# Attention scores on TensorE: the second matmul of two neighbouring key chunks on 64 rows each, in different halves of the array

## The chip, the cores and the metric

The kernel runs on one core of a Trainium2 chip. The metric is the device time of one execution in microseconds; lower is better. Before the change three runs took 1370.55 to 1374.48 us, median 1372.14 us. The profile shows one execution of its own, which took 1372.62 us.

## What is computed

The reference is one layer of a mixed encoder: a normalised input of 2048 tokens by 1024 channels, one input projection to 4364 columns, three groups that read it (a matrix-memory group of 4 heads, a forgetting attention of 4 heads with 64 channels each, a convolution group), a gate for each, an output projection, a residual and a final norm. The change lies in the attention:

```
cum    = cumsum(log_sigmoid(f_pre))                  # per head, over tokens
logits = q @ k.T * 64**-0.5 + cum[query] - cum[key]  # causal, 128-query blocks
p      = softmax(logits)
y      = p @ v
```

## The kernel before

The work is written per 512 tokens (`TB`), as blocks 0 to 3. For each block the input is normalised and transposed, and the projections run as matmuls whose operands are split in two parts, `hi` (the value in the matmul's 32-bit format `F32R`) and `lo` (what is left). Three products (hi hi, hi lo, lo hi) are added in PSUM. The weights are read again from DRAM for each block.

**How the attention's operands are laid out.** `unit_fqk` (line 382) projects q and k of a block, splits them into `hi` and `lo` and stores both to DRAM scratch, `q_d` and `k_d`. `k_d[head, part, 64, token]` holds for each head 64 rows of `hi` and then 64 rows of `lo`. `fox_load_qk` (line 813) reads back: a key chunk of 512 tokens is a tile of 128 rows, `hi` in rows 0 to 63 and `lo` in rows 64 to 127. The queries come as two tiles: `L["q", 0]` has q's `hi` twice, once in each half of the rows, and `L["q", 1]` has q's `lo` twice.

**The scores.** `fox_scores` (line 850) works on 128 queries (`qi`) of a pair of such blocks (`pr`) against all key chunks that they may see: 1 chunk for queries of block 0, up to 4 for block 3. For each chunk one PSUM tile `pq` receives two matmuls of 128 rows: L864 with q's `hi` (so hi hi + hi lo) and L865 with q's `lo` (so lo hi + lo lo). VectorE then adds the forgetting bias and keeps the running maximum (L872), which frees the PSUM tile, and GpSimd masks the bias of the chunk on the diagonal (L869). After the last chunk ScalarE takes the exponentials (L879). The diagonal chunk has only the columns that the queries can see, rounded up to at least 256.

`fox_scores` is a generator that yields once per chunk. `fox_run` (line 953) advances it one or two items ahead of `fox_apply` (line 887), which transposes the probabilities on TensorE (L918), splits them (L926, L927) and multiplies by the values (L905, L906). While the last projections of block 3 are made, `fox_run` is stepped from inside them (`bg_step`, line 267); afterwards it is the main loop, and the output projection `outproj` (L1063) is stepped from a counter (`FR`, line 1165) as filler. A planner with a cost model of its own then orders the instructions of each engine; among those that can run, those written earlier go first.

**PSUM.** Eight banks: pool `psp` has 3 (tag "p": `pq` of query blocks 2 and 3, and the output projection's `po`), `psx` has 2, `psm` has 3 (tag "m": `pq` of query blocks 0 and 1, and the transposes `ptr`).

Of the kernel before, what the change touches and what calls it, by code (L numbers as in the profile page):

```python
# [8 lines left out]
F32 = mybir.dt.float32  # L9
F32R = mybir.dt.float32r  # L10
AF = mybir.ActivationFunctionType
ALU = mybir.AluOpType
# [4 lines left out]
P = 128  # L17
S = 2048
# [3 lines left out]
TB = 512  # L22
# [5 lines left out]
NEG = -1e30  # L28
# [10 lines left out]
def tile_hybrid_trunk(  # L39
# [21 lines left out]
    v, s, g, pe, dma = nc.vector, nc.scalar, nc.gpsimd, nc.tensor, nc.sync  # L61
# [16 lines left out]
    k_d = scratch.tile([H, 2, 64, S], F32, name="k_d")  # L78
# [37 lines left out]
    psp = ps1.enter_context(tc.tile_pool(name="psp", bufs=PB[0], space=PSUM))  # L116
    psx = ps1.enter_context(tc.tile_pool(name="psx", bufs=PB[1], space=PSUM))
    psm = ps1.enter_context(tc.tile_pool(name="psm", bufs=PB[2], space=PSUM))
# [132 lines left out]
    def load_unit(name):  # L251
        if len(uready) < 2:
            prefetch()
        for _ in range(min(TP, len(backlog))):
            backlog.pop(0)()
        run_stage()
        if side:
            side.pop(0)()
        nm, w = uready.pop(0)
        assert nm == name  # L260
        return w
# [18 lines left out]
    def mm_cm(name, w, h, m):  # L280
        ps = proj_psum(f"pc_{name}")
        cs = slice(m * P, (m + 1) * P)
        n = 0
        for k in range(KT):
            wh, wl = w[0][k // 4][:, k % 4, cs], w[1][k // 4][:, k % 4, cs]
            for a, r in ((wh, h[0][k]), (wh, h[1][k]), (wl, h[0][k])):
                pe.matmul(ps, a, r, start=(n == 0), stop=(n == 3 * KT - 1))  # L287
                n += 1
            bg_step()
        return ps  # L290
# [91 lines left out]
    def unit_fqk(b, h, which):  # L382
        w = load_unit(f"f{which}{b}")
        for m in range(2):
            ps = mm_cm(f"f{which}{b}_{m}", w, h, m)
            lo = cpool.tile([P, 542], F32R, name=f"ql{which}{b}{m}", tag="c")[:, 0:TB]
            qf = lo.bitcast(F32)
            if which == 0:
                s.activation(qf, ps, AF.Identity, bias=colse[:, m : m + 1], scale=0.125)
            else:  # L390
                s.activation(qf, ps, AF.Identity, bias=cols[:, R_BFQ + 2 + m : R_BFQ + 3 + m])
            hi = cpool.tile([P, 542], F32R, name=f"qh{which}{b}{m}", tag="c")[:, 0:TB]
            s.copy(hi, qf)
            v.tensor_tensor(lo, qf, hi.bitcast(F32), op=ALU.subtract)
            bs = slice(b * TB, (b + 1) * TB)
            for e, t in enumerate((hi, lo)):
                if which == 0:
                    dma.dma_start(q_d[m, e, :, bs], t.bitcast(F32))
                else:
                    for a in range(2):  # L400
                        dma.dma_start(k_d[2 * m + a, e, :, bs], t[a * 64 : (a + 1) * 64, :].bitcast(F32))

    def silu2(name, ps, bcol, pool, tag, bufs):
        o = pool.tile([P, 542], F32, name=f"o_{name}", tag=tag, bufs=bufs)[:, 0:TB]
# [445 lines left out]
    def fox_scores(qd, hd, pr, L, out_):  # L850
        nk = qd * TB + (pr + 1) * 256
        nch = qd + 1
        for qi in range(2):
            t0 = qd * TB + pr * 256 + qi * P
            nm = f"{qd}{hd}{pr}{qi}"
            qs = slice(pr * 256 + qi * P, pr * 256 + (qi + 1) * P)
            mx = fpool.tile([P, 16], F32, name=f"mx{nm}", tag="mx", bufs=MXB)
            Sc = []
            for ch in range(nch):
                W = min(TB, nk - ch * TB)  # L860
                Wq = W if ch < qd else W - P * (1 - qi)
                pq = (psm if qd < PQM else psp).tile([P, 512], F32, name=f"pq{nm}{ch}", tag="m" if qd < PQM else "p")
                Wm = max(Wq, 256)
                pe.matmul(pq[:, 0:Wm], L["q", 0][:, qs], L["k", ch][:, 0:Wm], start=True, stop=False)  # L864
                pe.matmul(pq[:, 0:Wm], L["q", 1][:, qs], L["k", ch][:, 0:Wm], start=False, stop=True)  # L865
                nb = L["n", ch]
                if ch == qd:
                    nb = fpool.tile([P, TB], F32, name=f"nd{nm}", tag="nd", bufs=NDB)
                    g.affine_select(out=nb[:, 0:Wq], in_=L["n", ch][:, 0:Wq], pattern=[[-1, Wq]],  # L869
                                    compare_op=ALU.is_ge, fill=NEG, base=t0 - ch * TB, channel_multiplier=1)  # L870
                Sb = fpool.tile([P, TB], F32, name=f"S{nm}{ch}", tag="S", bufs=SB)
                v.tensor_tensor_reduce(  # L872
                    Sb[:, 0:Wq], pq[:, 0:Wq], nb[:, 0:Wq], 1.0,
                    NEG if ch == 0 else mx[:, ch - 1 : ch], ALU.add, ALU.max, mx[:, ch : ch + 1])
                Sc.append((Sb, Wq))
                yield
            v.tensor_scalar(mx[:, 4:5], mx[:, qd : qd + 1], -1.0, None, op0=ALU.mult)  # L877
            for ch, (Sb, Wq) in enumerate(Sc):
                s.activation(Sb[:, 0:Wq], Sb[:, 0:Wq], AF.Exp, bias=mx[:, 4:5], accum_out=mx[:, 8 + ch : 9 + ch])  # L879
            sm = mx[:, 8:9]  # L880
            if nch > 1:
                sm = mx[:, 5:6]
                v.reduce_sum(sm, mx[:, 8 : 8 + nch], axis=AX.X)
            v.reciprocal(mx[:, 6:7], sm)
            out_.append(([t for t, _ in Sc], mx))
# [62 lines left out]
    L, SH = {}, {}  # L948
# [4 lines left out]
    def fox_run(items, on_item=lambda i: None):  # L953
# [11 lines left out]
        def advance(i):  # L965
            load(nqk, fox_load_qk, min(i + (AH0 if items[min(i, len(items) - 1)][0] < 2 else AH), len(items) - 1 if free_hh else 15))
            if i < len(items) and i not in gens:
                qd, hp, hh, pr = items[i]
                ress[i] = []
                gens[i] = fox_scores(qd, hp * 2 + hh, pr, L[qd, hp, hh], ress[i])  # L970
# [106 lines left out]
    for b in range(NB):  # L1077
# [35 lines left out]
        if b < NB - 1:  # L1113
            unit_fz(b, h)
            conv_fin(b, h, accs)
            hn = hprep(b + 1)
            unit_fqk(b, h, 0)
            unit_fqk(b, h, 1)
            h = hn
# [10 lines left out]
    fpool = ctx.enter_context(tc.tile_pool(name="fpool", bufs=2, side="right"))  # L1130
# [5 lines left out]
    for k in range(EP):  # L1136
        prep_out(k)
    unit_fqk(b, h, 0)
    for k in range(EP, 4):
        prep_out(k)  # L1140
# [7 lines left out]
    def fillers():  # L1148
        for qd in range(NB):
            while ODONE[qd] not in marks:  # L1150
                yield
            yield from outproj(qd)

    fill = fillers()
    k = 4
    f = 0.0
# [21 lines left out]
NDB = 2  # L1178
SB = 12
# [9 lines left out]
PQM = 2  # L1189
# [49 lines left out]
```

## Time and profile before

| | |
|---|---|
| median of 3 runs | 1372.14 us |
| the profiled execution | 1372.62 us |
| its span in the profile | 1370.8 us |
| TensorE (PE) busy | 1278.7 us, 93% of the span, 7383 matmuls |
| weight loads (PEld) busy | 1112.9 us, 81% |
| VectorE (DVE) busy | 961.0 us, 70% |
| ScalarE (ACT) busy | 570.3 us, 42% |
| GpSimd (POOL) busy | 345.1 us, 25% |
| score matmuls L864 and L865 | 160 each, from 912.9 us to 1297.3 us |

A timeline row gives the start, the duration, the engine, the line, the tiles, the shape of the array used (rows * columns), the shape written and how many instructions were merged into the row. A matmul needs its weight load (PEld) first. Durations of matmuls overlap, since the array is pipelined: what one costs is the distance between two starts.

### The profile page before, as it was taken

What the parts mean: (1) busy time and instruction counts of PE and PEld (TensorE: products, weight loads), DVE (VectorE), ACT (ScalarE), POOL (GpSimd) and SP (SyncE); (2) the same over time, 40 slices, a digit from 0 to 9 for tenths busy, and PEclk for the clock granted to TensorE, in tenths of its full rate; (3) what the DMA queues carried; (4) which work ended last, traced back from release to release, by engine and by line L of the source; (5) the groups of instructions that cost most, each with busy time, mean ns of one, the idle gap of its engine ahead of it and who ended that gap; (6) DMA issues with size and microseconds to landing.
All of it is one profiled execution on the core that took longest, in us unless ns stands there. A gap on an engine that the chain in (4) does not pass through costs nothing. (4 is left out here: it accounts for less than half of the span.)

```text
span 1370.8 us, 21119 instructions
## 1 busy us (share of the span) xinstructions
PE 1278.7 (93%) x7383; PEld 1112.9 (81%) x7383; DVE 961.0 (70%) x2473; ACT 570.3 (42%) x1204; POOL 345.1 (25%) x398
## 2 busy tenths in 40 slices
PE   3747999999999999999999999998989999999997
PEld 2637898887889888989888889988868888878886
DVE  6789948748997655794662796674786677866742
ACT  4472434354233236330314232224575565655631
POOL 3466545510132010050110070121131211211121
PEclk9977999999999999999999999999999999999999
DMA  9947768699897469564558764469986454644141
GB/s 266 321 170 235 239 231 292 230 320 397 305 347 246 155 221 314 186 214 167 188 189 270 217 242 173 168 228 326 294 263 183 152 173 143 198 149 134 62 131 62
DMA packets 151874, 301.62 MB, mean 220 GB/s; under 512 B 14968, under 2 KB 92072, under 8 KB 133592
## 3 DMA queue, kind: packets, MB, share of 16 engines
q1 hardware_dynamic: 151768, 300.28, 65.4%
q8 instruction: 58, 0.95, 0.3%
q14 instruction: 48, 0.39, 0.1%
HBM read 224.54 MB, written 75.69 MB: 219 GB/s over the span
## 5 line engine op out<-in xcount | busy, mean ns | idle before, releaser
L461 DVE SCALAR_TENSOR_TENSOR ac<-ca,dww,ac 128x512 f32<-128x512 f32 x228 | 181.5, 831 | 2.4 <-ACT ac L446 1.9
L1063 PE MATMUL po<-wo,yh 128*128 128x512 f32 x512 | 164.7, 397 | 1.0 <-ACT yh L1053 0.7
L287 PE MATMUL pc_qk<-hh,w_qk 128*128 128x512 f32 x512 | 163.1, 395 | 0.3 <-DMA w_qk<-wd_qk 0.3
L299 PE MATMUL pt_mv<-w_mv,hh 128*128 128x256 f32 (+1 forms) x512 | 100.4, 297 | 29.2 <-ACT w_mv L181 10.5
L879 ACT ACTIVATE S<-S,mx 128x512 f32<-128x512 f32 (+3 forms) x160 | 103.7, 651 | 52.4 <-DVE mx L877 48.8
L287 PEld LDWEIGHTS pc_qk<-hh,w_qk 128*128 128x128 f32 x512 | 96.2, 188 | 21.0 <-DMA w_qk<-wd_qk 0.6
L1063 PEld LDWEIGHTS po<-wo,yh 128*128 128x128 f32 x512 | 94.1, 188 | 21.0 <-ACT yh L1053 0.9
L299 PEld LDWEIGHTS pt_mv<-w_mv,hh 128*128 128x128 f32 x512 | 84.7, 202 | 31.1 <-ACT w_mv L181 10.9
L927 DVE TENSOR_TENSOR tl<-ptr,th 128x512 fp32r<-128x512 f32 (+1 forms) x144 | 92.4, 654 | 24.7 <-ACT th L926 23.7
L1063 PE MATMUL po<-wo,ya 128*128 128x512 f32 x256 | 101.1, 396 | 0.0
L299 PE MATMUL pt_mo<-w_mo,hh 128*128 128x256 f32 x512 | 96.9, 290 | 4.3 <-DMA w_mo<-wd_mo 2.2
L287 PE MATMUL pc_qk<-hl,w_qk 128*128 128x512 f32 x256 | 100.8, 394 | 0.0
L926 ACT CAST th<-ptr 128x512 fp32r<-128x512 f32 (+1 forms) x144 | 76.3, 561 | 51.2 <-PE ptr L918 50.3
L552 DVE SCALAR_TENSOR_TENSOR am<-um,cols,am 128x512 f32<-128x512 f32 x96 | 83.4, 877 | 10.1 <-ACT am L549 9.3
L918 PE MATMUL ptr<-ident,S 128*128 128x128 f32 x544 | 84.1, 275 | 4.8 <-DVE tl L927 3.4
L299 PEld LDWEIGHTS pt_mo<-w_mo,hh 128*128 128x128 f32 x512 | 82.0, 196 | 4.8 <-DMA w_mo<-wd_mo 2.4
L287 PE MATMUL pc_f<-hh,w_f 128*128 128x512 f32 x256 | 84.8, 400 | 0.0
L869 POOL TENSOR_SCALAR_AFFINE_SELECT nd<-n 128x128 f32<-128x128 f32 (+1 forms) x64 | 30.5, 479 | 208.4 <-DVE mx L872 129.0
L287 PE MATMUL pc_mz<-hh,w_mz 128*128 128x512 f32 x256 | 82.7, 395 | 0.0
L299 PE MATMUL pt_mv<-w_mv,hl 128*128 128x256 f32 (+1 forms) x256 | 74.7, 293 | 0.0
L299 PE MATMUL pt_mo<-w_mo,hl 128*128 128x256 f32 x256 | 73.4, 289 | 0.0
L918 PEld LDWEIGHTS ptr<-ident,S 128*128 128x128 f32 x544 | 64.5, 142 | 10.1 <-DVE tl L927 2.8
(267 smaller groups left out, 3245.0 us busy)
## 6 DMA issues: line engine op xcount, KB each, us to landing
w_qk<-wd_qk SPq DMA_DIRECT2D x24, 1024.0 KB
w_mo<-wd_mo SPq DMA_DIRECT2D x12, 1024.0 KB
w_mz<-wd_mz SPq DMA_DIRECT2D x12, 1024.0 KB
w_f<-wd_f SPq DMA_DIRECT2D x12, 1024.0 KB
w_mv<-wd_mv SPq DMA_DIRECT2D x10, 1024.0 KB
n<-nb_d SPq DMA_DIRECT2D x36, 256.0 KB
wa<-in_w_ada_dram SPq DMA_DIRECT2D x16, 512.0 KB
x<-in_x_dram SPq DMA_DIRECT2D x16, 512.0 KB
```

The lines of the kernel that those rows point to most:

```text
L287: pe.matmul(ps, a, r, start=(n == 0), stop=(n == 3 * KT - 1))
L299: pe.matmul(ps[:, 0:width], a[:, cs], r, start=(n == 0), stop=(n == 3 * KT - 1))
L461: backlog.append(lambda acc=acc, u=u, i=2 * j + m, j=j: v.scalar_tensor_tensor(acc, u[:, j : j + TB], dww[:, i : i + 1], acc, op0=ALU.mult ...
L552: v.scalar_tensor_tensor(acc, u[:, j : j + TB], cols[:, r + 8 * j : r + 8 * j + 1], acc, op0=ALU.mult, op1=ALU.add)
L869: g.affine_select(out=nb[:, 0:Wq], in_=L["n", ch][:, 0:Wq], pattern=[[-1, Wq]], compare_op=ALU.is_ge, fill=NEG, base=t0 - ch * TB, channel ...
L879: s.activation(Sb[:, 0:Wq], Sb[:, 0:Wq], AF.Exp, bias=mx[:, 4:5], accum_out=mx[:, 8 + ch : 9 + ch])
L918: pe.transpose(pt[:, i, qi * P : (qi + 1) * P], Ps[qi][0][kk // TB][:, kk % TB : kk % TB + P], ident)
L926: s.copy(f(th), f(pt))
L927: v.tensor_tensor(f(tl), f(pt), f(th.bitcast(F32)), op=ALU.subtract)
L1063: pe.matmul(po, a, w[:, ns], start=(i == 0), stop=(i == 3 * KT - 1))
```

## The change

Two things change.

- In `unit_fqk` the keys of odd blocks are stored with the parts exchanged: `lo` in rows 0 to 63 and `hi` in rows 64 to 127. For even blocks nothing changes.
- In `fox_scores` the chunks are taken two at a time. First both chunks get their matmul with q's `hi` on all 128 rows, as before. Then both get their second matmul, now on only the 64 rows that hold the key's `hi` part: rows 0 to 63 for the even chunk, rows 64 to 127 for the odd one. These two use different halves of the array's rows and different PSUM tiles. The product lo lo is left out there. A chunk without a partner (the only chunk of query block 0, the third of block 2) keeps both matmuls of 128 rows. The mask, the bias and the maximum of both chunks follow after all four matmuls, with one yield each as before.

```diff
@@ unit_fqk
-                        dma.dma_start(k_d[2 * m + a, e, :, bs], t[a * 64 : (a + 1) * 64, :].bitcast(F32))
+                        dma.dma_start(k_d[2 * m + a, e ^ (b % 2), :, bs], t[a * 64 : (a + 1) * 64, :].bitcast(F32))
@@ fox_scores
-            for ch in range(nch):
-                W = min(TB, nk - ch * TB)
-                Wq = W if ch < qd else W - P * (1 - qi)
-                pq = (psm if qd < PQM else psp).tile([P, 512], F32, name=f"pq{nm}{ch}", tag="m" if qd < PQM else "p")
-                Wm = max(Wq, 256)
-                pe.matmul(pq[:, 0:Wm], L["q", 0][:, qs], L["k", ch][:, 0:Wm], start=True, stop=False)
-                pe.matmul(pq[:, 0:Wm], L["q", 1][:, qs], L["k", ch][:, 0:Wm], start=False, stop=True)
-                nb = L["n", ch]
...
-                yield
+            for c0 in range(0, nch, 2):
+                grp = []
+                for ch in range(c0, min(c0 + 2, nch)):
+                    W = min(TB, nk - ch * TB)
+                    Wq = W if ch < qd else W - P * (1 - qi)
+                    pq = (psm if qd < PQM else psp).tile([P, 512], F32, name=f"pq{nm}{ch}", tag="m" if qd < PQM else "p")
+                    Wm = max(Wq, 256)
+                    pe.matmul(pq[:, 0:Wm], L["q", 0][:, qs], L["k", ch][:, 0:Wm], start=True, stop=False)
+                    grp.append((ch, Wq, Wm, pq))
+                for ch, Wq, Wm, pq in grp:
+                    r = slice(0, P) if len(grp) == 1 else slice(64 * (ch % 2), 64 * (ch % 2) + 64)
+                    pe.matmul(pq[:, 0:Wm], L["q", 1][r, qs], L["k", ch][r, 0:Wm], start=False, stop=True)
+                for ch, Wq, Wm, pq in grp:
+                    nb = L["n", ch]
...
+                    yield
```

The lines left out (mask, bias, maximum) are the same on both sides.

More of the change, by code (lines that the diff above doesn't have):

```diff
@@ L858, in fox_scores @@
             Sc = []
-            for ch in range(nch):
-                W = min(TB, nk - ch * TB)
-                Wq = W if ch < qd else W - P * (1 - qi)
-                pq = (psm if qd < PQM else psp).tile([P, 512], F32, name=f"pq{nm}{ch}", tag="m" if qd < PQM else "p")
-                Wm = max(Wq, 256)
-                pe.matmul(pq[:, 0:Wm], L["q", 0][:, qs], L["k", ch][:, 0:Wm], start=True, stop=False)
-                pe.matmul(pq[:, 0:Wm], L["q", 1][:, qs], L["k", ch][:, 0:Wm], start=False, stop=True)
-                nb = L["n", ch]
[L867 to L875, printed above, removed]
-                yield
@@ new lines, in fox_scores @@
+            for c0 in range(0, nch, 2):
[12 more added lines that the diff above has]
+                    nb = L["n", ch]
+                    if ch == qd:
+                        nb = fpool.tile([P, TB], F32, name=f"nd{nm}", tag="nd", bufs=NDB)
+                        g.affine_select(out=nb[:, 0:Wq], in_=L["n", ch][:, 0:Wq], pattern=[[-1, Wq]],
+                                        compare_op=ALU.is_ge, fill=NEG, base=t0 - ch * TB, channel_multiplier=1)
+                    Sb = fpool.tile([P, TB], F32, name=f"S{nm}{ch}", tag="S", bufs=SB)
+                    v.tensor_tensor_reduce(
+                        Sb[:, 0:Wq], pq[:, 0:Wq], nb[:, 0:Wq], 1.0,
+                        NEG if ch == 0 else mx[:, ch - 1 : ch], ALU.add, ALU.max, mx[:, ch : ch + 1])
+                    Sc.append((Sb, Wq))
+                    yield
```

## The prediction

> **What bounds the kernel now.** First the busy time of each engine, then the same by stretches of the part that the change touches.
>
> ```profile
> span 1370.8 us, 21119 instructions
> PE 1278.7 (93%) x7383; PEld 1112.9 (81%) x7383; DVE 961.0 (70%) x2473; ACT 570.3 (42%) x1204; POOL 345.1 (25%) x398
> ```
> ```profile
> 950.00:1000.00 50.00, 46.35 (x276) 39.41 (x275) 34.21 (x126) 29.03 (x76) 10.26 (x31) 0.97 0.88 280
> 1000.00:1050.00 50.00, 44.98 (x256) 36.47 (x256) 39.23 (x138) 31.68 (x83) 15.19 (x29) 1.00 0.70 218
> 1050.00:1100.00 50.00, 50.00 (x298) 43.71 (x297) 33.49 (x96) 28.83 (x73) 9.32 (x17) 1.00 0.57 175
> 1100.00:1150.00 50.00, 49.34 (x298) 43.15 (x297) 36.56 (x110) 29.12 (x74) 10.58 (x21) 1.00 0.59 175
> 1200.00:1250.00 50.00, 46.77 (x274) 40.92 (x273) 33.41 (x94) 27.30 (x70) 6.74 (x13) 0.97 0.43 130
> 1250.00:1300.00 50.00, 49.66 (x297) 43.24 (x296) 35.77 (x99) 30.19 (x75) 8.72 (x15) 1.00 0.34 103
> ```
>
> The columns are PE, PEld, DVE, ACT, POOL, then the granted clock, the DMA share and GB/s. TensorE is busy for 45 to 50 us of every 50 at full clock, VectorE for 33 to 39. What TensorE waits for between 1000 and 1300 us, by the view of waits, and the last long step of the chain that ends last:
>
> ```profile
> PE pq L864 <- DVE mx L872: 4.8, 5, 2.8
> PE pa L905 <- ACT th L926: 1.4, 3, 0.6
> PE ptr L918 <- DVE tl L927: 1.1, 2, 1.0
> ```
> ```profile
> 1324.05 39.62 PE po L1063 x171
> ```
>
> These three are 7.3 us in 300. From 1000 us to the end the kernel is a queue of matmuls, and the last of them end it: a microsecond more or less of TensorE work in the scores is nearly a microsecond of time. The chain's row also prices a matmul of 512 columns in that queue: 39.62 / 171 = 0.232 us.
>
> **What the change removes.** The number of matmuls and loads stays: 160 of L864, 160 of L865.
>
> ```profile
> L865 PE MATMUL pq<-k,q x112: 274/393/632, 1021.6 to 1297.3; 128*128 128x512 f32 x88, 128*128 128x256 f32 x16, 128*128 128x384 f32 x8
> L865 PE MATMUL pq<-kv,q x48: 277/389/522, 913.1 to 1029.9; 128*128 128x512 f32 x24, 128*128 128x256 f32 x16, 128*128 128x384 f32 x8
> ```
>
> A set of 128 queries occurs 16 times per query block (4 heads, 2 `pr`, 2 `qi`). Block 0 has no pair, block 1 has one per set, block 2 one (its third chunk is single), block 3 two: 64 pairs. In 32 of them both chunks are full; in the 32 of chunks (0,1) of block 1 and (2,3) of block 3 the second is the diagonal one, 256 columns wide in 16, 384 in 8, 512 in 8. If both halves run at once, the shorter matmul of the pair disappears. Its price by width, from starts that follow each other:
>
> ```profile
> 1122.67 0.28 PE L906 MATMUL pa<-tl,v 128*128 128x256 f32 x1
> 1122.79 0.28 PE L905 MATMUL pa<-th,v 128*128 128x256 f32 x1
> ```
> ```profile
> 963.60 0.34 PE L864 MATMUL pq<-kv,q 128*128 128x384 f32 x1
> 963.78 0.34 PE L865 MATMUL pq<-kv,q 128*128 128x384 f32 x1
> ```
>
> So 0.12 us and 0.18 us. Removed at most: 40 x 0.232 + 8 x 0.18 + 16 x 0.12 = **12.6 us**. The halves still need a load each. In the row of four loads below, 0.47 us with 0.14 for the last, loads follow each other by 0.11 us. If the upper half's load comes after the lower half's, its matmul starts up to 0.11 us late: nothing is lost with a partner of 256 columns (0.11 + 0.12 = 0.23), 0.06 with 384, 0.11 with 512, together 40 x 0.11 + 8 x 0.06 = 4.9 us. I take that loss, since nothing else is ahead of the two loads to hide them (next part): **7.7 us removed**, bounds 0 (the halves run one after the other) and 12.6.
>
> **What it adds: changing the rows in use, twice per pair.** No score matmul of before uses 64 rows. But the trace has one instruction on fewer than 65 rows inside a busy stretch, a transpose of 62 rows (L793), between one of 74 rows and projection matmuls of 128:
>
> ```profile
> 62.76 0.14 PEld L792 LDWEIGHTS pt_cols<-ident,r 74*128 74x128 f32 x1
> 62.87 0.23 PE L792 MATMUL pt_cols<-ident,r 74*128 74x74 f32 x1
> 63.03 0.14 PEld L793 LDWEIGHTS pt_cols<-ident,r 62*128 62x128 f32 x1
> 63.03 0.27 PE L793 MATMUL pt_cols<-ident,r 62*128 62x62 f32 x1
> 63.23 0.30 PEld L299 LDWEIGHTS pt_v<-w_v,hl 128*128 128x128 f32 x2
> 63.23 0.51 PE L299 MATMUL pt_v<-w_v,hl 128*128 128x268 f32 x2
> 63.46 0.31 PEld L299 LDWEIGHTS pt_v<-w_v,hh 128*128 128x128 f32 x2
> 63.58 0.41 PE L299 MATMUL pt_v<-w_v,hh 128*128 128x268 f32 x2
> 63.82 0.28 PE L299 MATMUL pt_v<-w_v,hl 128*128 128x268 f32 x1
> ```
>
> For comparison four transposes of 128 rows in the same surroundings, and four of 96 rows:
>
> ```profile
> 60.71 0.47 PEld L146 LDWEIGHTS xT<-ident,x 128*128 128x128 f32 x4
> 60.82 0.60 PE L146 MATMUL xT<-ident,x 128*128 128x128 f32 x4
> 61.17 0.37 PE L299 MATMUL pt_v<-w_v,hl 128*128 128x268 f32 x1
> 61.38 0.41 PE L299 MATMUL pt_v<-w_v,hh 128*128 128x268 f32 x2
> ```
> ```profile
> 108.31 0.41 PEld L377 LDWEIGHTS pg<-ident,T 96*128 96x128 f32 x4
> 108.41 0.49 PE L377 MATMUL pg<-ident,T 96*128 96x96 f32 x4
> ```
>
> With 74, 96 and 128 rows the load starts 0.10 to 0.11 us before its matmul, under the one in front. The load of 62 rows doesn't: it starts at 63.03, 0.16 us after L792 began. The next load of 128 rows doesn't either: it starts at 63.23, and its matmul takes 0.23 us (to the next load at 63.46) where two later ones take 0.24 together. So TensorE seems to empty before it goes from 128 rows to 64, and again on the way back, and each time the next load stands uncovered. It could be that L793 waited for its data; but that transfer (`r` from `c_dw_w`) was issued long before, and the late load behind it has no such reason:
>
> ```profile
> 49.56 1.05 SPq L757 DMA_DIRECT2D r<-in_c_dw_w_dram  x1
> ```
>
> The price of going there and back, from 62.87 to 63.46 = 0.59 us for three matmuls: upper bound, against matmuls that follow each other by their columns alone (0.232 / 512 = 0.45 ns each, 136 columns 0.06, and 0.12 for the 268 columns): 0.59 - 0.18 = 0.41 us. Lower bound, against transposes and the matmul after them (0.35 / 4 = 0.09 each, then 61.17 to 61.38 = 0.21): 0.59 - 0.39 = 0.20 us. The pair goes from a projection-like matmul of 512 columns to another, so it is nearer to the upper case; behind it there is often a transpose, so not all of it. I take 0.35 us: 64 x 0.35 = **22.4 us**, bounds 12.8 and 26.2.
>
> The Trainium skill, "TensorEngine Tiling (Array Packing)", section Tiling Modes, Key Properties, says that changing the tiling mode, not just the tile, drains TensorE; the rows around L793 agree, and by that rule the sum is the one above. "TensorE: Matmul & The Clock Gate", Part 3, describes matmuls on different row groups that start about 4 ns apart and names no price for entering; by that page alone the result would be the first rival below.
>
> **Order and buffers.** The four matmuls of a pair now need two PSUM banks before the first second matmul runs; for query blocks 2 and 3 `po` holds the third of that pool, for block 1 `ptr` shares it. Behind an L864 that waits stand TensorE's transposes, L905 and L1063, and behind those ACT's L926 and DVE's L927. Today's waits for a bank are the 4.8 us above. I take no addition, bounds 0 and +5 (as many again), since `po` fills such gaps. VectorE gets both reductions at once, the first about 0.6 us later; DVE has 11 to 17 us free in each 50 and scores run an item ahead, so 0. The exchanged rows of `k_d` are the same stores and loads of the same size: 0.
>
> **Sum.** 22.4 - 7.7 = +14.7 us of TensorE work. A quarter of the pairs (block 1, whose keys come from the tile `kv`) lies before 1030 us, where TensorE is free 7 to 10% of the time, so I let 13 us arrive. On the profiled 1372.6 that is 1385.6; the median is 0.5 lower: **1385 us**. Its own range: from 12.8 - 12.6 = 0 to 26.2 - 0 = 26 us, of which 24 arrive in the same share: 1372 to 1396.
>
> **Rivals.**
> *Faster: changing rows is free and the halves run together.* The loads of the pair hide as all others do, and the 12.6 us are gained, some 11 of them at the end: 1361. For it: matmuls are the bound, and the trace has no pair on separate rows. Against it: the two late loads around L793. It decides below 0.12 to 0.2 us per there-and-back (7.7 or 12.6 divided by 64), where the gain is used up.
> *No change: 64 rows cost what 128 cost.* The halves run one after the other and the change of rows is free or is just paid by the overlap: 1372, give or take 4. For it: a load of 62 rows takes the 0.14 us that one of 74 takes, so fewer rows are not faster by themselves.
> *Much slower: the halves are separated.* The planner puts other matmuls between instructions that are written together:
>
> ```profile
> 973.46 0.28 PE L864 MATMUL pq<-kv,q 128*128 128x256 f32 x1
> 973.58 0.28 PE L905 MATMUL pa<-th,kv 128*128 128x256 f32 x1
> 973.69 0.28 PE L865 MATMUL pq<-kv,q 128*128 128x256 f32 x1
> ```
>
> A pair torn apart pays twice and saves nothing: 0.70 instead of 0.23 us. With half of the pairs torn, 32 x 0.47 = 15 us more: 1400. For it: two banks at once of three, so the second L864 may come late and the first half run alone. Against it: the neighbours are mostly together in the rows I read.
>
> **How the numbers follow.** Forecast 0.55, faster rival 0.20, no change 0.10, torn pairs 0.15. A measurement can tell 0.3%, 4 us, from nothing; about a tenth of the forecast's own chance falls inside that, a little of it and of the no-change rival below. Faster 0.22, same 0.14, slower 0.64. The range holds the forecast's own, reaches the faster rival, and ends two microseconds under the middle of the torn one: 1360 to 1398.
>
> **What would show it.** In the changed trace the second matmuls read 64*128. Right, if the load of the first half starts after its L864 has streamed and not with it, if the two halves start within 0.11 us, and if the next load of 128 rows is late again, with 1.1 to 1.2 us from the first matmul of a full pair to the next instruction where four took 0.93. Wrong, if those loads start ahead of time and the pair takes 0.7 us, or if the halves stand apart. The forecast also falls if waits for `mx` in front of L864 grow by much more than 5 us.

## The result and the profile after

The changed kernel took 1403.49 us in the median of 5 runs (1402.43 to 1406.59), the one before 1372.24 us: a ratio of 1.0229, interval 1.0214 to 1.0245. It is **31 us slower**; 13 us slower was forecast, with 1398 as the upper end. The busy time per engine, on the page of the changed kernel:

```profile
span 1401.9 us, 21109 instructions
PE 1316.9 (94%) x7383; PEld 1109.8 (79%) x7383; DVE 968.2 (69%) x2473; ACT 571.0 (41%) x1204; POOL 345.6 (25%) x398
```

TensorE has the same 7383 matmuls and is busy for 1316.9 - 1278.7 = 38 us more; the other engines have what they had. By stretches it is now busy without a break, with fewer matmuls in the same time (274 to 298 per 50 us in the stretches quoted of before from 1050 us on, 263 to 284 now):

```profile
1050.00:1100.00 50.00, 49.95 (x269) 39.22 (x268) 33.16 (x95) 27.41 (x71) 9.85 (x18) 1.00 0.51 156
1100.00:1150.00 50.00, 50.00 (x284) 40.18 (x284) 35.90 (x103) 27.65 (x70) 11.14 (x20) 1.00 0.58 164
1150.00:1200.00 50.00, 50.00 (x263) 38.22 (x262) 36.35 (x98) 27.91 (x72) 10.43 (x17) 1.00 0.55 161
1250.00:1300.00 50.00, 50.00 (x265) 38.12 (x263) 31.08 (x83) 26.46 (x68) 7.86 (x13) 1.00 0.39 121
```

The waits that TensorE had in front of L864 didn't grow. Its view of waits in the changed kernel has, over the whole span, only this for the first matmuls of the scores (now L866) on `mx`:

```profile
PE pq L866 <- DVE mx L878: 0.5, 1, 0.5
```

So the time went into the matmuls themselves. One stretch of TensorE's timeline shows how. L866 are the first matmuls, L870 the second ones:

```profile
1122.07 0.36 PE L911 MATMUL pa<-th,v 128*128 128x256 f32 x1
1122.27 0.40 PE L866 MATMUL pq<-k,q 128*128 128x512 f32 x1
1122.60 0.49 PE L870 MATMUL pq<-k,q 64*128 64x512 f32 x1
1123.02 0.50 PE L866 MATMUL pq<-k,q 128*128 128x512 f32 x1
1123.45 0.50 PE L870 MATMUL pq<-k,q 64*128 64x512 f32 x1
1123.88 0.39 PE L912 MATMUL pa<-tl,v 128*128 128x256 f32 x1
1124.10 0.28 PE L911 MATMUL pa<-th,v 128*128 128x256 f32 x1
```

The source writes L866, L866, L870, L870. The planner put L866, L870, L866, L870: the pair is **torn apart**. The four matmuls take 1122.27 to 1123.88 = 1.61 us, where four took 4 x 0.232 = 0.93. Counted over the whole trace, 11 of the 64 pairs stand together and 53 don't, so TensorE makes 53 x 2 + 11 = 117 visits to 64 rows. A visit is one or more 64-row matmuls between matmuls of 128 rows. The weight loads of the same stretch (in brackets the idle time before one and what ended it; `issue` is time in which it waited for nothing that the profile shows):

```profile
1122.15 0.19 PEld L866 LDWEIGHTS pq<-k,q 128*128 128x128 f32 x1
1122.59 0.18 PEld L870 LDWEIGHTS pq<-k,q 64*128 64x128 f32 x1 [0.25 <-issue]
1123.02 0.19 PEld L866 LDWEIGHTS pq<-k,q 128*128 128x128 f32 x1 [0.24 <-issue]
1123.45 0.18 PEld L870 LDWEIGHTS pq<-k,q 64*128 64x128 f32 x1 [0.25 <-issue]
1123.88 0.19 PEld L912 LDWEIGHTS pa<-tl,v 128*128 128x128 f32 x1 [0.24 <-DVE mx L878]
```

At every change the load starts with its matmul (on all 117 visits within 0.04 us of it, on the way in and on the way back) and not 0.1 us or more ahead of it. It was so around L793 in the trace of before. One of the pairs that stand together:

```profile
1073.66 0.61 PE L866 MATMUL pq<-k,q 128*128 128x512 f32 x2
1074.21 0.50 PE L870 MATMUL pq<-k,q 64*128 64x512 f32 x2
1074.64 0.73 PE L1069 MATMUL po<-wo,yh 128*128 128x512 f32 x2
1075.21 0.39 PE L1069 MATMUL po<-wo,ya 128*128 128x512 f32 x1
```

Two second matmuls take the 0.50 us of one: the halves do run at once (in all 11 such pairs they start 3 to 4 ns apart). Even so, 1073.66 to 1074.64 = 0.98 us, and the next two matmuls take 0.57 instead of 0.46.

### The profile page after: what moved, and what is told of

Read it like the earlier page. It is cut to its first block, busy times and chain, and to the rows that moved or that the text cites. A ratio compares the mean times of both kernels' runs of the same rounds, so it can differ in the third digit from the quotient of the medians.

```text
span 1401.9 us, 21109 instructions
## 1 busy us (share of the span) xinstructions
PE 1316.9 (94%) x7383; PEld 1109.8 (79%) x7383; DVE 968.2 (69%) x2473; ACT 571.0 (41%) x1204; POOL 345.6 (25%) x398
## 4 chain that ended last, share of the span: by engine, by line
PE 78%; DVE 9%; DMA 7%; SPq 2%; ACT 2%; issue 1%; POOL 0%; DVEq 0%; POOLq 0%; ACTq 0%
PE po L1069 13%; PE pc_qk L287 11%; PE pc_f L287 6%; PE pt_mo L299 6%; PE pc_mz L287 5%; PE pt_mv L299 5%; PE ptr L924 4%; PE pq L870 3%; PE pc_cz L287 3%; DVE ac L461 3%; PE pc_fz L287 3%; PE pa L911 2%; PE pa L912 2%; PE pc_ca L287 2%; PE pq L866 2%; PE pt_v L299 2%
## 5 line engine op out<-in xcount | busy, mean ns | idle before, releaser
L1069 PE MATMUL po<-wo,yh 128*128 128x512 f32 x512 | 169.0, 404 | 1.7 <-ACT yh L1059 1.7
```

The costliest lines, as they stand in the source:

```text
L1069: pe.matmul(po, a, w[:, ns], start=(i == 0), stop=(i == 3 * KT - 1))
```

## The experiments

Theory A: each change between 128 and 64 rows empties TensorE and leaves a load uncovered, and there are 117 because the pairs are torn. Theory B (rival B in the expectations): the order is to blame, with two banks wanted at once. The runs measure the late loads and their price; that TensorE empties is inferred from them. Times are medians; the ratio is to the kernel before on the same chips.

**The order without the change of rows.**

```diff
-                    r = slice(0, P) if len(grp) == 1 else slice(64 * (ch % 2), 64 * (ch % 2) + 64)
+                    r = slice(0, P)
```

> The changed kernel with its order kept (two chunks at a time, keys of odd blocks exchanged, 53 of 64 pairs torn apart by the planner) but every second matmul on all 128 rows, lo lo included. Theory A (each change between 128 and 64 rows empties TensorE, and 117 of them make the loss): without any such change the time is that of the kernel before, 1372 within 4 us. Rival B (the loss comes from the order: two banks wanted at once, bunched matmuls, the planner's other order): the loss stays, 1395 to 1405.

1371.4 us, ratio 1.0003 (0.9989 to 1.0017). Grouping, order and exchanged keys cost nothing; theory B falls for the changed kernel. TensorE of this run is busy for

```profile
PE 1277.8 (93%) x7383; PEld 1110.8 (81%) x7383; DVE 964.6 (70%) x2473; ACT 570.5 (42%) x1204; POOL 343.2 (25%) x398
```

The changed kernel has the same order on TensorE, matmul by matmul in the two traces, and 1316.9 - 1277.8 = 39.1 us more. With the 11 whole pairs saving some 0.2 us each (12.6 / 64), that is (39.1 + 2.2) / 117 = 0.35 us per change there and back.

**The change of rows without the order.** From the kernel before:

```diff
-                pe.matmul(pq[:, 0:Wm], L["q", 1][:, qs], L["k", ch][:, 0:Wm], start=False, stop=True)
+                r = slice(0, P if ch == qd and qd % 2 == 0 else 64)
+                pe.matmul(pq[:, 0:Wm], L["q", 1][r, qs], L["k", ch][r, 0:Wm], start=False, stop=True)
```

> The kernel before with its order and key storage; only the 128 second matmuls that have a partner in the changed kernel use rows 0 to 63 (lo lo left out there), each alone, none overlapping another: 128 changes there and back and nothing saved. Theory A: if one costs 0.28 us at the end (33 us / 117 in the changed kernel) +36 us, 1408; if the 0.41 us of the trace's starts arrive in full, +52, 1424. Rival B (order and banks): the order is the old one, so 1372. Third possibility, 64 rows cost what 128 do: 1372.

1401.16 us, ratio 1.0222 (1.0190 to 1.0254): +30 us. The page:

```profile
span 1405.1 us, 21112 instructions
PE 1325.7 (94%) x7383; PEld 1112.3 (79%) x7383; DVE 967.3 (69%) x2473; ACT 570.7 (41%) x1204; POOL 343.8 (24%) x398
```

TensorE gains 47.0 us of work, 47.0 / 128 = 0.37 us per change. The span of this execution, the slowest of the four (1406.85 us), grew by 34.3 us; the other 13 went into gaps that TensorE had (92 us without work before, 79 here). The median came out below both of theory A's numbers (1408 and 1424): of the 47.0 us only 30, 65%, arrived. The rival and the third possibility, 1372, both fall.

**All pairs together.** The second matmuls are put behind the last first one, in issue order only:

```diff
-                    pe.matmul(pq[:, 0:Wm], L["q", 0][:, qs], L["k", ch][:, 0:Wm], start=True, stop=False)
+                    m1 = pe.matmul(pq[:, 0:Wm], L["q", 0][:, qs], L["k", ch][:, 0:Wm], start=True, stop=False)
...
+                with tc.issue_after(m1.ins):
```

> The changed kernel; the second matmuls of a pair are also ordered behind the first matmul of its second chunk, so that all 64 pairs stand together (64 changes there and back instead of 117). Theory A: 64 x 0.28 to 0.41 = 18 to 26 us, less at most 12.6 for the overlap: 1378 to 1386, still slower than before. Rival C (the trace's two whole pairs mislead, halves that stand together gain what they were meant to): 1360. Rival B (banks): the same or slower than the changed kernel, 1403 or more, since a pair now always waits for two banks.

1385.28 us, ratio 1.0106 (1.0083 to 1.0128). All 64 pairs stand together in the trace, and by the ratios 17 us of the 31 are gone (21 in the repeat below); it is still slower than before. Rival C falls: a pair with its halves at once doesn't pay for the change.

The same kernel ran once more beside the group of four below:

> The run with the pairs together once more, beside the group of four on the same chip, so that 4 to 6 us can be told: 1385 within 3 us.

1384.18 us, ratio 1.0078 (1.0054 to 1.0103). TensorE's busy time differs by 3.7 us between the profiled executions of these two runs of one kernel, on two chips (1292.3 and 1288.6), so a difference in its work is known to about 4 us.

**Together, on the same half.** As before it, but keys are not exchanged and

```diff
+                        r = slice(0, P) if len(grp) == 1 else slice(0, 64)
```

> As the run with all pairs together, but keys are not exchanged and both second matmuls use rows 0 to 63, the same half, so they cannot run at once; the number of changes is the same 64. Theory A with real overlap in the changed kernel: 12.6 us slower than the run with the pairs together on different halves, 1390 to 1398. If the two halves do not overlap in time at all: the same time as that run, within 3 us.

1394.84 us, ratio 1.0166 (1.0136 to 1.0196): 9.6 us more than on different halves. First the matmuls on different halves:

```profile
1123.40 0.39 PE L866 MATMUL pq<-k,q 128*128 128x512 f32 x1
1123.71 0.50 PE L871 MATMUL pq<-k,q 64*128 64x512 f32 x2
1124.14 0.38 PE L912 MATMUL pa<-th,v 128*128 128x256 f32 x1
1124.37 0.28 PE L913 MATMUL pa<-tl,v 128*128 128x256 f32 x1
```

then on the same half:

```profile
1153.98 0.63 PE L866 MATMUL pq<-k,q 128*128 128x512 f32 x2
1154.53 0.73 PE L871 MATMUL pq<-k,q 64*128 64x512 f32 x2
1155.19 0.38 PE L912 MATMUL pa<-th,v 128*128 128x256 f32 x1
```

The visit takes 0.43 us in the first and 0.66 in the second; the difference, 0.23, is a whole matmul of 512 columns. Over all pairs the median visit is 0.43 us against 0.66 where the second chunk has 512 columns (40 pairs), 0.43 against 0.60 with 384 (8) and 0.42 against 0.54 with 256 (16): 12.5 us in all, of which 9.6 arrive. The loads, first on different halves, then on the same:

```profile
1123.71 0.19 PEld L871 LDWEIGHTS pq<-k,q 64*128 64x128 f32 x2 [0.24 <-issue]
```
```profile
1154.53 0.29 PEld L871 LDWEIGHTS pq<-k,q 64*128 64x128 f32 x2 [0.36 <-issue]
```

On different halves two loads take the 0.19 us of one. The first timeline also gives the price in steps: 0.31 from L866 to the visit (0.08 over 0.232), 0.43 for the visit (0.20 over), 0.23 for the first matmul behind it (0.11 over the 0.12 of 256 columns), together 0.39 us.

**The enforced order on 128 rows.** As the run with all pairs together, with `r = slice(0, P)`.

> The order of the run with all pairs together (both second matmuls behind both first ones), but on all 128 rows, lo lo included: no change of rows. It measures what the enforced order and its wait for two banks cost by themselves. Theory A (the 14.5 us of that run are 64 changes less the overlap): 0 to 3 us, 1371 to 1375. If the enforced order costs 6 us or more, a change of rows is cheaper than the 0.35 us that the trace gives.

1376.47 us, ratio 1.0026 (1.0012 to 1.0040): +4 us, just above theory A's 0 to 3 and under the 6 that would have made a change of rows cheaper. Against this run the changes of rows on the same half cost 1394.84 - 1376.47 = 18.4 us of time (19 by the ratios, since the two ran on different chips); in TensorE's work (1302.7 on its page, 1280.2 here) 22.5 / 64 = 0.35 us each.

```profile
PE 1302.7 (93%) x7383; PEld 1107.6 (79%) x7383; DVE 964.2 (69%) x2473; ACT 571.0 (41%) x1204; POOL 345.3 (25%) x398
```
```profile
PE 1280.2 (93%) x7383; PEld 1110.7 (81%) x7383; DVE 960.8 (70%) x2473; ACT 571.8 (42%) x1204; POOL 344.2 (25%) x398
```

**96 rows instead of 64.** As the run with 64 rows alone, with 96 in place of 64.

> As the run with 64 rows alone (old order, old key storage, +30 us there), but the same 128 second matmuls use rows 0 to 95: hi and half of lo (half of lo lo left out). Theory A as the trace of before has it (going under 65 rows empties TensorE, 96 rows does not): 1371 within 3 us, and loads ahead of their matmuls. Rival (any number of rows other than 128 does it): +30 us, 1401.

1371.97 us, ratio 0.9996 (0.9977 to 1.0015). The loads stay ahead of their matmuls, 1119.89 before 1120.12:

```profile
1119.89 0.19 PEld L866 LDWEIGHTS pq<-k,q 96*128 96x128 f32 x1
1120.12 0.40 PE L866 MATMUL pq<-k,q 96*128 96x512 f32 x1
1120.12 0.42 PEld L1064 LDWEIGHTS po<-wo,yh 128*128 128x128 f32 x2
```

So not every matmul on fewer than 128 rows costs this; going from 128 to 64 and back does. Where between 96 and 64 the limit lies, no run here measures.

**Two pairs per visit.** From the run with all pairs together, its order behind the last first matmul included: for query block 3 all four chunks are a group, the odd ones with banks of the transposes' pool.

```diff
-            for c0 in range(0, nch, 2):
+            for c0 in range(0, nch, 4 if qd == 3 else 2):
...
-                for ch in range(c0, min(c0 + 2, nch)):
+                for ch in range(c0, min(c0 + (4 if qd == 3 else 2), nch)):
...
-                    pq = (psm if qd < PQM else psp).tile([P, 512], F32, name=f"pq{nm}{ch}", tag="m" if qd < PQM else "p")
+                    lo = qd < PQM or (qd == 3 and ch % 2)
+                    pq = (psm if lo else psp).tile([P, 512], F32, name=f"pq{nm}{ch}", tag="m" if lo else "p")
```

> As the run with pairs together, but for query block 3 all four chunks are one group: four first matmuls, then two pairs of second matmuls in one visit to 64 rows; the odd chunks' banks there come from the transposes' pool, since four are needed. 48 changes instead of 64, the same overlap. Theory A: 16 x 0.24 to 0.38 = 4 to 6 us faster than the pairs together, 1379 to 1382, still slower than before. If waits for four banks decide: slower than the pairs together, 1387 or more.

1410.36 us, ratio 1.0280 (1.0248 to 1.0312), the slowest of all. The visit itself is as it should be, four matmuls in 1197.83 - 1197.16 = 0.67 us:

```profile
1197.16 0.73 PE L872 MATMUL pq<-k,q 64*128 64x512 f32 x4
1197.83 0.39 PE L914 MATMUL pa<-tl,v 128*128 128x256 f32 x1
```

Yet TensorE now stands idle for parts of the stretches of block 3, where the changed kernel kept it busy throughout:

```profile
1150.00:1200.00 50.00, 47.83 (x260) 38.41 (x258) 31.76 (x87) 26.52 (x66) 9.85 (x16) 0.97 0.43 132
1200.00:1250.00 50.00, 41.71 (x209) 32.89 (x210) 30.42 (x80) 26.07 (x65) 10.01 (x15) 0.86 0.49 154
1250.00:1300.00 50.00, 46.06 (x258) 36.45 (x256) 30.10 (x80) 24.33 (x62) 6.01 (x11) 1.00 0.34 110
```

The same on 128 rows (`r = slice(0, P)`):

> The order and the banks of the run with groups of four, but every second matmul on all 128 rows, lo lo included: no change of rows and no overlap. If the loss of that run (+38 us) is order and banks (four banks wanted at once, two of them from the transposes), nearly all of it stays: 48 changes at 0.36 us less 12.6 us are +5, so 1400 to 1408. If the four-matmul visits to 64 rows themselves are dear, it falls to 1372 to 1380.

1404.45 us, ratio 1.0238 (1.0212 to 1.0263). So +33 of the +38 us are the order with its four banks, and 6 are the changes less the overlap, for which +5 was expected. The split is approximate: the trace with 64 rows has 49 visits, not 48, since the second matmuls of one group of four stand in two places, and the orders of the two traces differ in 27 of 7383 places. Which of the two, order or banks, makes the 33 was not taken apart. No version here is faster than the kernel before.

## Why the prediction missed

**What bounds the kernel: right in kind.** Of 39.1 us of added work, 32.1 arrived (1403.49 - 1371.4), 82%; the forecast let 13 of 14.7 through, 88%. With 64 rows alone less arrived, 65%. With the pairs together, against the same order on 128 rows, 1384.18 - 1376.47 = 7.7 us arrived of 8 to 12 us of work (1288.6 or 1292.3, less 1280.2).

**The price of going to 64 rows and back: right.** 0.35 us was taken, between 0.20 and 0.41, from a single transpose of 62 rows. Three comparisons of TensorE's work give 0.35, 0.37 and 0.35; the steps in one timeline give 0.39. With 4 us of uncertainty in the work, the price is known to 0.03 us over 117 or 128 visits and to 0.06 over 64. The choice of 0.35 within these bounds was a judgement from one example. Whether L793 waited for its data no longer matters, since every visit to 64 rows shows the same late loads.

**The late load of the upper half: wrong.** It was to cost 4.9 us. The loads of the two halves run side by side (0.19 us for two). The overlap was worth 9.6 us at the end and 1302.7 - 1292.3 = 10.4 us of TensorE's work (1292.3 on the page of the run with pairs together; 14.1 by the repeat's 1288.6), where 7.7 was taken and 12.6 was the bound. The sign that was asked for, 1.1 to 1.2 us for a full pair, came out as 0.98, since the second half isn't late. (One slip in the sum: at the share of 13 in 14.7, 26 us are 23 and not 24.)

```profile
PE 1292.3 (93%) x7383; PEld 1100.6 (80%) x7383; DVE 961.7 (70%) x2473; ACT 571.3 (41%) x1204; POOL 346.9 (25%) x398
```

**The number of changes: this is the step that failed.** The sum counts 64 changes, one per pair, and so forecasts 1385 us for a kernel whose pairs stand together. That kernel takes 1385.28 and 1384.18 us. That the figure is met so closely is in part luck: the late load was not there, so that the change of rows cost 7.7 us against the same order on 128 rows and not 13, and the stated order added 4 us that the sum had at 0. In the changed kernel the planner tore 53 of 64 pairs, so there were 117. The prediction had this as its third rival, with half of the pairs torn (+15 us) and a chance of 0.15, since "the neighbours are mostly together in the rows I read". Those rows were of before, where a second matmul stands directly behind its own first one (155 of 160 in that trace), the neighbour that it also has in the torn order; they said nothing of two chunks' second matmuls. By the prediction's own price, 53 x (0.70 - 0.23) = 25 us on top of the 14.7 are 40 us of work; 39 were measured.

**Why it tears them** is open. The prediction's reason was a bank that comes late. On the chip banks come late by little: with all pairs kept together, TensorE waits between 930 and 1330 us in front of the first matmuls mainly for these two, 3.8 us in all.

```profile
PE pq L866 <- DVE mx L879: 2.6, 7, 0.5
PE pq L866 <- ACT po L1074: 1.2, 3, 0.7
```

But the planner goes by a cost model of its own. By the rule given with the kernel, the second L866 stands behind L870 only if that model held that it could not run yet; what the model held is not on record.

**Order and buffers: right.** 0 was taken and the ratio is 1.0003; where the order is enforced it costs 4 us, inside the bound of 5.

**The rivals.** Faster: the halves run at once as that rival said, but the change isn't free; its own limit of 0.12 to 0.2 us per change is passed. No change: excluded by the ratios of the runs with 64 rows. Much slower: this is what happened, with 53 pairs torn in place of 32.

## What to carry to other kernels

Count visits, not pairs: using half of the array's rows pays only if what is saved per visit (0.23 us for two matmuls of 512 columns) is more than the way there and back (0.35 to 0.39 us), so one pair per visit between matmuls of 128 rows loses. By the steps above, two full pairs per visit would take 0.67 + 0.08 + 0.11 = 0.86 us where 128 rows take 4 x 0.232 = 0.93. This is an estimate: the one run that did it lost 33 us to the order and banks that it needed. Instructions that must stand next to each other need a stated order where a planner lays them out, and the number of times that they do can be counted in the trace. An unusual shape that occurs once in the trace, here a small transpose in the set-up, can price an edit that nothing else in the trace shows.

## What was not expected of the hardware

96 rows cost nothing (ratio 0.9996), 64 rows 0.35 us per visit. The weight loads of two matmuls on different halves run at the same time (0.19 us for two, 0.29 on the same half). And behind a wait TensorE can be slow for a while: in the kernel with groups of four, matmuls of 256 columns behind a wait of 2.29 us start 0.21 us apart instead of 0.12. The granted clock there is 0.55, where it was 1.00 in the 4 us up to 1199; that the wait caused this is not shown.

```profile
1202.21 0.72 PE L867 MATMUL pq<-k,q 128*128 128x512 f32 x1 [2.29 <-DMA k<-k_d]
1202.73 0.41 PE L914 MATMUL pa<-tl,v 128*128 128x256 f32 x1
1202.94 0.41 PE L913 MATMUL pa<-th,v 128*128 128x256 f32 x1
1203.15 0.41 PE L914 MATMUL pa<-tl,v 128*128 128x256 f32 x1
```
```profile
1195.00:1199.00 4.00, 4.00 (x29) 3.21 (x27) 3.23 (x6) 1.68 (x4) 0.35 (x2) 1.00 0.16 39
1202.20:1206.00 3.80, 3.79 (x14) 3.02 (x14) 2.03 (x3) 2.40 (x7) 3.04 (x3) 0.55 1.03 331
```
